# A decoder block in split fp32: weight preparation held back before three norms, transposes under the first loads, and pairs of matmuls in turned order

## Chip, core and metric

The kernel runs on one core of a Trainium2 chip. The metric is the device time of one execution in microseconds; three executions of the kernel before were timed, and one more was profiled. The engines are TensorE (PE in the profile, with its weight loads as PEld), VectorE (DVE), ScalarE (ACT), GpSimd (POOL) and SyncE (SP), which issues most of the DMAs. Each engine works through its own list of instructions in the order in which they were written.

## What is computed

One decoder block for 256 tokens of 2048 channels, all in fp32. Cut to its core, the reference is:

```
x = layer_norm(ALPHA * x + 0.5 * swiglu(x, ffn1_w_gate, ffn1_w_up, ffn1_w_down), ln1_g, ln1_b)
mix = hybrid_mixer(x, ...)            # x @ w_in, RG-LRU and dilated attention, @ w_out
x = layer_norm(ALPHA * x + mix, ln2_g, ln2_b)
x = layer_norm(ALPHA * x + 0.5 * swiglu(x, ffn2_w_gate, ffn2_w_up, ffn2_w_down), ln3_g, ln3_b)
x = x + sigmoid(x @ w_ple_gate) * (p @ w_ple_proj)
```

The hidden width of swiglu is 5632. There are three layer norms, and behind each of them a new large product starts that needs the normed x.

## The kernel before

**Split products.** Every large product is made of fp32r matmuls on split operands: a weight tile of 256 x 512 (an *entry* of the plan, `plan[q]`) is loaded as `raw`, ACT casts it to `hi` (L104), DVE subtracts to get `lo` (L109). The activations are split in the same way (`xT[:, :, 0]` and `xT[:, :, 1]`). An entry is 1.05 us of work on ACT and 1.2 us on DVE.

**Two forms of product.** With the weight stationary (`mm_stationary_w`), each 128 x 128 block gives a *pair*: `hi` against 512 columns (both halves of xT) and `lo` against 256. With the activations stationary (`mm_moving_w`), each block gives three matmuls of 512 columns.

**The plan.** `take` hands out the next entry; `advance` prepares entries ahead, at most 7 beyond those taken (`AHEAD`), at most `SLOTS` = 7 live at once, and never beyond `self.limit`. An entry that is marked `work` gets its `hi` and `lo` in the pool `work` (11 buffers, tag `w4`) and needs no slot. Two entries in `down_last` (`plan[-6:-4]`, those of its n = 1) and the first three entries behind each boundary are marked so. `advance` emits the cast of an entry, and its subtraction one entry later.

**A boundary.** `down_last` ends a stage. It makes its four column blocks n = 0..3 for the first 128 tokens (t = 0), where DVE adds each into `acc` (L385) and takes its statistics (`ln_stats`, L513), then `ln_norm(st[0], 0)` norms the first half (aggregate, a power on POOL, four scalings at L525). The four blocks for t = 1 follow on PE; in the middle of the one with n = 1, the first four normed blocks are transposed (`ln_transpose(0, 0)`, L535), and further transposes stand behind n = 1, 2 and 3. ACT scales and casts what was transposed (L538, L64), DVE subtracts (L65). Then the next stage starts on the first 128 tokens, with the transposes of the second half behind its entries j = 4 to 7 (`HOOKS`). The boundaries are here called LN1 (about 700 us), LN2 (about 1071 us) and LN3 (about 1780 us).

**The entries behind a boundary** are prepared while `down_last` takes its own. They are called W1, W2 and W3 below: they appear in the trace as `w<-raw` on ACT and `w<-raw,w` on DVE, in contrast to the `hi<-raw` and `lo<-raw,hi` of the entries in slots.

**The mixer.** In `group_a` the weight is stationary; between its entries `tick` steps the generators `lru` and `attention`, which put small groups of plain fp32 matmuls and transposes into PE's stream.

**The start.** SP loads the pieces of x and the first entries of `ffn1_w_gate`; POOL writes the identity for the transposes in `setup`.

Of the kernel before, what the change touches and what calls it, by code (L numbers as in the profile page):

```python
# [12 lines left out]
P = 128  # L13
D = 2048
S = 256
KB = D // P
# [24 lines left out]
class Block:  # L41
# [119 lines left out]
    def make_plan(self):  # L161
        i = self.i
        plan = self.plan = []

        def add(w, r0, c0, n=1, **kw):
            for j in range(n):
                plan.append({"src": self.rows2(w, r0 + 256 * j, c0), "work": False,
                             "parts": [slice(0, 2)], "stationary": False, **kw})

        def ffn(name):  # L170
            g, u, d = (i[f"{name}_w_{v}"] for v in ("gate", "up", "down"))
            todo = []
            for c in range(NCH):
                for w in (g, u):
                    for j in range(8):
                        add(w, 256 * j, c * 512, stationary=c > 0 or name == "ffn1")
                        if j % 2 and todo:
                            todo.pop(0)()
                if c % 2:
                    todo = blocks(d, (c - 1) * 512, 0)  # L180
                    if c < NCH - 2:
                        todo += blocks(d, (c - 1) * 512, 2)
            for n in (2, 3):
                add(d, (NCH - 3) * 512, n * 512, 4)
            last_down(d, (NCH - 1) * 512)

        def last_down(w, r0):
            down(w, r0)
            for e in plan[-6:-4]:
                e["work"] = True  # L190

        def blocks(w, r0, n):
            got = {}

            def entries(kind):
                for j in range(2):
                    entry(kind, j)

            def entry(kind, j):
                r, c = r0 + 256 * j, n * 512  # L200
                b22, b21 = self.rows2(w, r + 512, c + 512), self.rows2(w, r + 512, c)
                at = {"p2": (512, 0), "p3": (512, 512)}.get(kind, (0, 0))
                add(w, r + at[0], c + at[1], kind=kind)
                e = got[kind, j] = plan[-1]
                p1 = got["p1", j]
                if kind == "p1":
                    e["beside"] = self.rows2(w, r, c + 512)
                    e["after"] = [lambda: self.raw_sum(p1["raw"], p1["other"]), lambda: self.raw_grow(p1["other"], b22)]
                elif kind == "p3":
                    e["after"] = [lambda: self.raw_sum(p1["raw"], e["raw"])]  # L210
                elif kind == "p6":
                    e["after"] = [lambda: self.raw_grow(p1["raw"], b21)]
                if kind in ("p5", "p6", "p4", "p7"):
                    e["of"] = p1, "other" if kind == "p7" else "raw"

            return [lambda kind=kind: entries(kind) for kind in ORDER]

        def down(w, r0):
            for n in range(4):
                add(w, r0, n * 512, 2)  # L220

        w, wo = i["w_in"], i["w_out"]
        ffn("ffn1")
        for j in range(8):
            plan[j]["load"] = lambda j=j: self.load_x(j)
            plan[j]["split"] = lambda j=j: self.split_x(j)
            plan[16 + j]["load"] = lambda j=j: self.load_acc(j)
        plan[0]["parts"] = [slice(0, 1), slice(1, 2)]
        v0 = len(plan)
        add(w, 0, QW + KVW, 8)  # L230
        for g in range(3):
            add(w, 0, C_X + g * 512, 8, stationary=True)
        for h in range(4):
            add(w, 0, h * 512, 8)
        for g in range(3):
            add(w, 0, C_Y + g * 512, 8, stationary=True)
            down(wo, g * 512)
        last_down(wo, 3 * 512)
        f0 = len(plan)
        ffn("ffn2")  # L240
        p0 = len(plan)
        for n in range(4):
            add(i["w_ple_proj"], 0, n * 512)
        q = len(plan)
        for n in range(4):
            add(i["w_ple_gate"], 0, n * 512, 8)
        for e in plan[q + 6:q + 8] + plan[-2:]:
            e["work"] = True
        for q in (v0, f0, p0):
            for e in plan[q:q + 3]:  # L250
                e["work"] = True
        plan[p0]["load"], plan[p0]["split"] = self.load_p, self.split_p
        self.xraw = {}
        self.limit = len(plan)
        self.loaded = self.ready = self.ready_lo = self.taken = self.live = 0
        self.ticks = 0
        self.lru_q, self.att_q, self.gate_q, self.res_q, self.form_q = [], [], [], [], []

    def rows2(self, w, r0, c0):
# [3 lines left out]
    def mm(self, out, lhsT, rhs, start, stop):  # L263
        self.nc.tensor.matmul(out, lhsT=lhsT, rhs=rhs, start=start, stop=stop, skip_group_check=True)  # L264

    def mm_stationary_w(self, bank, b, hi, lo, k, kb, tok, start, stop):
        bv = bank.rearrange("p (s t) -> p s t", s=2)
        c = slice(b * P, (b + 1) * P)
        self.mm(bv[:, :, tok], hi[:, k, c], self.xT[:, kb, :, tok], start, False)
        self.mm(bv[:, 0, tok], lo[:, k, c], self.xT[:, kb, 0, tok], False, stop)  # L270

    def mm_moving_w(self, bank, act, hi, lo, start, stop):
        ah, al = act
# [8 lines left out]
    def tokens_a(self, e, j, banks, tok, first, on_block=None):  # L282
        for b in range(4):
            for k in range(2):
                kb = 2 * j + k
                self.mm_stationary_w(banks[b], b, e["hi"], e["lo"], k, kb, tok, kb == 0 and first, kb == KB - 1)
            if on_block and j == 7:
                on_block(b, banks[b])

# [201 lines left out]

    def down_last(self, acts):
        es, st = [], [self.tile(self.small, [P, 4, 6], F32, "bst") for _ in range(2)]
        for n in range(4):
            es.append([self.take(), self.take()])
            self.down_mm(acts, es[n], 0, n, False)
            self.ln_stats(st[0], 0, n)
        self.ln_norm(st[0], 0)
        for n in range(4):
            self.down_mm(acts, es[n], 1, n, False, mid=(lambda: self.ln_transpose(0, 0)) if n == 1 else None)  # L500
            self.ln_stats(st[1], 1, n)
            if n < 3:
                for e in es[n]:
                    self.done(e)
            if n > 0:
                self.ln_transpose(0, n)
        self.ln_norm(st[1], 1)
        for e in es[3]:
            self.done(e)
# [130 lines left out]
    def setup(self):  # L640
        nc, i = self.nc, self.i
        c = self.const
        self.ident = c.tile([P, P], F32, name="ident")
        make_identity(nc, self.ident)
        self.mhalf = c.tile([P, 1], F32, name="mhalf")
        nc.gpsimd.memset(self.mhalf, -0.5)
        self.par = c.tile([P, 192], F32, name="par")
        self.trig = c.tile([P, 2, 2, 16], F32, name="trig")
        self.dec = c.tile([P, 2, 12], F32, name="dec")
# [56 lines left out]
    def lru(self, g, xb):  # L706
        nc, i = self.nc, self.i
# [17 lines left out]
        for b in range(4):  # L725
            gb = 4 * g + b
            bank = self.bank()
            self.mm(bank[:, :256], wr[:, b, :], xc[:, b, :], True, True)
            self.mm(bank[:, 256:], wi[:, b, :], xc[:, b, :], True, True)
            nc.scalar.activation(r[:, b, :], bank[:, :256], AF.Sigmoid, bias=self.par[:, 60 + gb:61 + gb])  # L730
            nc.scalar.activation(ig[:, b, :], bank[:, 256:], AF.Sigmoid, bias=self.par[:, 72 + gb:73 + gb])
            if b % 2:
                yield
        nc.gpsimd.tensor_tensor(ig, ig, xc, op=ALU.mult)
        th = self.wide()
# [38 lines left out]
    def attention(self, h, qks):  # L774
        nc = self.nc
# [30 lines left out]
        for t in range(2):  # L806
            nc.vector.tensor_reduce(mxs[t], prs[t][:, :, :(t + 1) * P], AX.XY, ALU.max)
            nc.vector.tensor_scalar(mxs[t], mxs[t], -SCALE, None, op0=ALU.mult)
        yield
        for t in range(2):  # L810
            pv = prs[t][:, :, :(t + 1) * P]
# [13 lines left out]
        nc.tensor.transpose(bank[:, 2 * P:3 * P], ps[1][:, P:], self.ident)  # L825
        pT = self.tile(self.qk, [P, 3 * P], F32, "qk")
        nc.scalar.copy(pT, bank[:, :3 * P])
        yield
        ob = self.bank()
        hc = slice(h * P, (h + 1) * P)  # L830
# [1 line left out]
        self.mm(ob[:, P:2 * P], self.v[:, 0, hc], pT[:, P:2 * P], True, False)  # L832
        self.mm(ob[:, P:2 * P], self.v[:, 1, hc], pT[:, 2 * P:], False, True)
        nc.scalar.copy(self.att[0][:, h, :], ob[:, :256])
        yield
        nc.vector.tensor_tensor(self.att[1][:, h, :], ob[:, :256], self.att[0][:, h, :].bitcast(F32), op=ALU.subtract)

# [12 lines left out]
    def mixer(self):  # L850
        nc = self.nc
# [7 lines left out]
        for h in range(4):  # L859
# [5 lines left out]
                qks.append(qk)  # L865

            self.group_b(on_bank)
            if h == 0:
                self.att = (self.wide_r(), self.wide_r())
            self.att_q.append(self.attention(h, qks))  # L870
# [138 lines left out]
```

## Time and profile before

| what | value |
|---|---|
| timed runs | 1912.32 us median of 3 (1910.5 to 1912.78) |
| profiled execution | 1905.79 us, of which 1904.0 us from its first to its last instruction |
| PE busy | 1868.5 us, 98% of the span, 9844 matmuls |
| DVE busy | 1494.9 us, 79% |
| ACT busy | 1077.8 us, 57% |
| POOL busy | 124.2 us, 7% |
| TensorE's granted clock | 0.995 of full speed over the span |

The profile is of one execution, and the time of that execution stands beside its span; the 1.79 us between them lie around the instructions. Ends of matmuls are modelled, so the starts are the better guide. A wait is written as idle time in brackets with the engine and line that ended it.

### The profile page before, as it was taken

The numbers are of one execution on the slowest core, as the hardware profiler recorded it, in microseconds if no ns is written. First come the engines' busy times: TensorE is split into PE (matmuls) and PEld (weight loads), VectorE is DVE, ScalarE is ACT, GpSimd is POOL, SyncE is SP. The second block draws the span as 40 slices with busy tenths as digits, with TensorE's granted clock in tenths as the row PEclk, the third lists the DMA queues.
The fourth block names the chain that finished last, engine by engine and source line by source line (L and its number), as shares of the span: only waits on it lengthen the run. The fifth ranks groups of instructions, "written<-read, shape, count | busy, mean of one in ns | idle before, by whom it ended". The sixth has DMA issues, their size and how long they took to land.

```text
span 1904.0 us, 26424 instructions
## 1 busy us (share of the span) xinstructions
PE 1868.5 (98%) x9844; PEld 1603.2 (84%) x9844; DVE 1494.9 (79%) x1910; ACT 1077.8 (57%) x1422; POOL 124.2 (7%) x108
## 2 busy tenths in 40 slices
PE   8999999999999989999999899999999999999899
PEld 7888888888888878887888788888888888888687
DVE  6698887887888876688677867878879888788674
ACT  6565555555655646555755455655556556556552
POOL 0001010100010000011100000101000101010000
PEclk9999999999999999999999999999999999999999
DMA  9678687788786857565455575887887878778381
GB/s 354 232 198 264 203 257 235 207 260 247 211 255 209 266 178 231 175 185 158 138 184 187 167 243 155 250 231 211 258 247 207 255 211 253 243 198 276 131 263 44
DMA packets 214593, 413.02 MB, mean 217 GB/s; under 512 B 13104, under 2 KB 15808, under 8 KB 214464
## 3 DMA queue, kind: packets, MB, share of 16 engines
q1 hardware_dynamic: 193856, 370.42, 58.1%
q0 software_dynamic: 20608, 40.91, 12.6%
q8 instruction: 77, 1.26, 0.3%
q14 instruction: 52, 0.43, 0.1%
HBM read 409.18 MB, written 2.10 MB: 216 GB/s over the span
## 4 chain that ended last, share of the span: by engine, by line
PE 95%; DVE 2%; ACT 1%; issue 1%; DMA 0%; SPq 0%; POOL 0%; DVEq 0%; POOLq 0%; ACTq 0%
PE mm L264 94%; DVE lo L109 1%; PE mm L535 1%; DMA raw<-in_ffn_w_gate_dram 0%; ACT hi L104 0%; DVE w L109 0%; DVE bst L513 0%; DVE acc L385 0%; PE mm L792 0%; DVE raw L82 0%; DVE w L721 0%; DVE w L65 0%; ACT w L64 0%; POOL rs L522 0%; DVE w L627 0%
## 5 line engine op out<-in xcount | busy, mean ns | idle before, releaser
L104 ACT CAST hi<-raw 128x1024 fp32r<-128x1024 f32 (+1 forms) x774 | 797.2, 1049 | 556.4 <-PE mm L264 501.2
L264 PE MATMUL mm<-xT,hi 128*128 128x512 f32 x3072 | 1057.6, 391 | 5.6 <-ACT hi L104 5.6
L109 DVE TENSOR_TENSOR lo<-raw,hi 128x1024 fp32r<-128x1024 f32 (+1 forms) x774 | 915.2, 1221 | 93.4 <-ACT hi L104 84.5
L264 PE MATMUL mm<-xT,lo 128*128 128x256 f32 x3072 | 850.5, 277 | 0.1
L264 PEld LDWEIGHTS mm<-xT,hi 128*128 128x128 f32 x3072 | 577.5, 188 | 127.2 <-ACT hi L104 5.8
L264 PEld LDWEIGHTS mm<-xT,lo 128*128 128x128 f32 x3072 | 577.7, 188 | 6.3 <-DVE lo L109 1.3
L264 PE MATMUL mm<-hi,w 128*128 128x512 f32 x1480 | 481.6, 391 | 1.8 <-DVE acc L435 1.2
L264 PEld LDWEIGHTS mm<-hi,w 128*128 128x128 f32 x1480 | 277.9, 188 | 63.7 <-ACT hi L104 1.5
L264 PE MATMUL mm<-lo,w 128*128 128x512 f32 x740 | 289.5, 391 | 0.0
L264 PE MATMUL mm<-hi,xT 128*128 128x512 f32 (+1 forms) x648 | 200.9, 385 | 0.0
L264 PEld LDWEIGHTS mm<-lo,w 128*128 128x128 f32 x740 | 139.1, 188 | 23.9
L85 POOL DMA_DIRECT2D raw<-in_ffn_w_down_dram x72 | 86.6, 1214 | 1080.7 <-DVE raw L82 547.7
L437 DVE TENSOR_TENSOR acc<-acc,mm 128x512 f32<-128x512 f32 x110 | 75.2, 684 | 98.6 <-PE mm L264 98.6
L264 PEld LDWEIGHTS mm<-hi,xT 128*128 128x128 f32 x648 | 120.3, 188 | 23.1
L264 PE MATMUL mm<-lo,xT 128*128 128x512 f32 (+1 forms) x324 | 123.6, 382 | 0.0
L378 DVE TENSOR_TENSOR w<-mm,w 128x256 f32<-128x256 f32 x192 | 80.2, 419 | 20.5 <-ACT w L377 20.0
L82 DVE TENSOR_TENSOR raw<-raw,raw 128x1024 f32<-128x1024 f32 x72 | 87.9, 1221 | 1.2
L377 ACT COPY w<-mm 128x256 f32<-128x256 f32 x192 | 69.6, 364 | 21.2 <-PE mm L264 17.2
L64 ACT CAST w<-qk 128x512 fp32r<-128x512 f32 (+1 forms) x42 | 25.5, 609 | 86.4 <-DVE qk L482 46.0
L612 ACT ACTIVATE w<-w 128x256 f32<-128x256 f32 x84 | 35.1, 418 | 66.3 <-DVE w L378 66.3
L264 PEld LDWEIGHTS mm<-lo,xT 128*128 128x128 f32 x324 | 61.0, 188 | 11.2
L613 DVE TENSOR_TENSOR w<-w,w 128x256 f32<-128x256 f32 x84 | 35.8, 426 | 41.4 <-ACT w L612 41.4
(139 smaller groups left out, 788.0 us busy)
## 6 DMA issues: line engine op xcount, KB each, us to landing
raw<-in_ffn_w_up_dram SPq DMA_DIRECT2D x176, 512.0 KB, 4.9
raw<-in_ffn_w_down_dram SPq DMA_DIRECT2D x176, 512.0 KB, 5.3
raw<-in_ffn_w_gate_dram SPq DMA_DIRECT2D x175, 512.0 KB, 6.0
raw<-in_w_in_dram SPq DMA_DIRECT2D x88, 512.0 KB, 4.6
raw<-in_ffn_w_down_dram POOLq DMA_DIRECT2D x72, 512.0 KB, 7.6
raw<-in_w_out_dram SPq DMA_DIRECT2D x32, 512.0 KB, 4.4
raw<-in_w_ple_gate_dram SPq DMA_DIRECT2D x32, 512.0 KB, 5.6
w<-in_ln_g_dram SPq DMA_DIRECT2D x12, 256.0 KB, 7.4
```

What stands on the lines that cost most here:

```text
L64: self.nc.scalar.copy(hi, src)
L82: self.nc.vector.tensor_tensor(a, a, b, op=ALU.add)
L85: self.nc.gpsimd.dma_start(a, src, accum_op=ALU.add)
L104: self.nc.scalar.copy(e["hi"][:, k, :], e["raw"][:, k, :])
L109: self.nc.vector.tensor_tensor(e["lo"][:, k, :], e["raw"][:, k, :], e["hi"][:, k, :].bitcast(F32), op=ALU.subtract)
L264: self.nc.tensor.matmul(out, lhsT=lhsT, rhs=rhs, start=start, stop=stop, skip_group_check=True)
L377: self.nc.scalar.copy(c, bank[:, 256:])
L378: self.nc.vector.tensor_tensor(dst, bank[:, :256], c, op=ALU.add)
L437: self.nc.vector.tensor_tensor(a, a, bank, op=op)
L535: nc.tensor.transpose(bank[:, q * P:(q + 1) * P], self.acc[:, t, kb * P:(kb + 1) * P], self.ident)
L612: nc.scalar.activation(s, g, AF.Sigmoid)
L613: nc.vector.tensor_tensor(g, g, s, op=ALU.mult)
```

## The change

Three edits are independent of each other.

- In `down_last` the limit of the plan is set to ten entries from the one taken first (its own eight and two behind the boundary) until the norm of the first token half has been emitted; then it is set back.
- In `setup`, eight transposes of the identity into a PSUM bank that nothing reads are issued to PE ahead of everything else.
- In the mixer, a flag `turn` is set behind each group of fp32 matmuls in `lru` and behind three of the four groups of `attention`; the next pair with the weight stationary (and not the first of its bank) is then issued with `lo` first and `hi` second. The flag is dropped where a `group_b` ends.

```
+        self.limit = self.taken + 10
         for n in range(4):
             es.append([self.take(), self.take()])
             self.down_mm(acts, es[n], 0, n, False)
             self.ln_stats(st[0], 0, n)
         self.ln_norm(st[0], 0)
+        self.limit = len(self.plan)
...
         make_identity(nc, self.ident)
+        bank = self.bank()
+        for _ in range(8):
+            nc.tensor.transpose(bank[:, :P], self.ident, self.ident)
...
-        self.mm(bv[:, :, tok], hi[:, k, c], self.xT[:, kb, :, tok], start, False)
-        self.mm(bv[:, 0, tok], lo[:, k, c], self.xT[:, kb, 0, tok], False, stop)
+        high = bv[:, :, tok], hi[:, k, c], self.xT[:, kb, :, tok]
+        low = bv[:, 0, tok], lo[:, k, c], self.xT[:, kb, 0, tok]
+        one, two = (low, high) if turn else (high, low)
+        self.mm(*one, start, False)
+        self.mm(*two, False, stop)
...
-                self.mm_stationary_w(banks[b], b, e["hi"], e["lo"], k, kb, tok, kb == 0 and first, kb == KB - 1)
+                turn = self.turn and kb > 0
+                self.mm_stationary_w(banks[b], b, e["hi"], e["lo"], k, kb, tok, kb == 0 and first, kb == KB - 1, turn)
+                if turn:
+                    self.turn = False
```

On DVE, at LN1, the instructions around the first norm stand in this order before (`w_1283`, `w_1287` and `w_1290` are the `lo` of W1, W2 and W3, `acc<-acc,mm` are the additions of n = 1, 2 and 3, and `BN_AGGR` begins the norm):

```order
L109 TENSOR_TENSOR w_1283_6572<-raw_6505,w_1282_6571 128x1024
L109 TENSOR_TENSOR w_1287_6593<-raw_6523,w_1286_6592 128x1024
L385 TENSOR_TENSOR acc<-acc,mm_6602 128x512
L513 BN_STATS bst_6561<-acc 128x6
L109 TENSOR_TENSOR w_1290_6599<-raw_6541,w_1289_6598 128x1024
L385 TENSOR_TENSOR acc<-acc,mm_6623 128x512
L513 BN_STATS bst_6561<-acc 128x6
L385 TENSOR_TENSOR acc<-acc,mm_6638 128x512
L513 BN_STATS bst_6561<-acc 128x6
L518 BN_AGGR mv_6653<-bst_6561 128x2
L520 TENSOR_SCALAR ve_6655<-mv_6653 128x1
L525 TENSOR_SCALAR acc<-acc,mv_6653,rs_6657 128x512 x4
```

With the change the same stretch of DVE's list, from the statistics of n = 2 on, reads as follows (`w_1288` is the `lo` of W2, `w_1298` that of W3):

```order
L521 BN_STATS bst_6570<-acc 128x6
L391 TENSOR_TENSOR acc<-acc,mm_6635 128x512
L521 BN_STATS bst_6570<-acc 128x6
L526 BN_AGGR mv_6650<-bst_6570 128x2
L528 TENSOR_SCALAR ve_6652<-mv_6650 128x1
L533 TENSOR_SCALAR acc<-acc,mv_6650,rs_6654 128x512 x4
L391 TENSOR_TENSOR acc<-acc,mm_6660 128x512
L521 BN_STATS bst_6571<-acc 128x6
L109 TENSOR_TENSOR w_1288_6602<-raw_6532,w_1287_6601 128x1024
L109 TENSOR_TENSOR w_1298_6678<-raw_6550,w_1297_6677 128x1024
L109 TENSOR_TENSOR lo_6684<-raw_6572,hi_6683 128x1024
L109 TENSOR_TENSOR lo_6690<-raw_6578,hi_6689 128x1024
```

The subtractions of W2 and W3 have moved from between the additions of the first token half to behind the norm and the first addition of the second half. It is the same at LN2 and LN3. The lists of ACT, SP and POOL keep their order everywhere.

On PE, in the mixer's first group behind the fp32 matmuls of `lru` (`mm<-w,w`, 128x256), the stream before and now:

```order
L264 MATMUL mm_7394<-w_1403_7234,w_1402_7231 128x256 x2
L264 MATMUL mm_7399<-w_1403_7234,w_1402_7231 128x256 x2
L264 MATMUL mm_7205<-xT,hi_7227 128x512
L264 MATMUL mm_7205<-xT,lo_7228 128x256
L264 MATMUL mm_7205<-xT,hi_7227 128x512
L264 MATMUL mm_7205<-xT,lo_7228 128x256
```

```order
L264 MATMUL mm_7403<-w_1404_7243,w_1403_7240 128x256 x2
L264 MATMUL mm_7408<-w_1404_7243,w_1403_7240 128x256 x2
L264 MATMUL mm_7214<-xT,lo_7237 128x256
L264 MATMUL mm_7214<-xT,hi_7236 128x512 x2
L264 MATMUL mm_7214<-xT,lo_7237 128x256
```

One pair has its two matmuls exchanged, so that two of 512 columns follow each other once. This happens at six places of the stream: behind the three groups of `lru` matmuls that fall among pairs, and behind three groups of `attention`, all for the last head. The eight transposes of the identity are the first work of PE.

## Rows read from the trace of the kernel before

**Rows 1.** The page: the chain that ended last, shares of the span.

```profile
PE 95%; DVE 2%; ACT 1%; issue 1%; DMA 0%; SPq 0%; POOL 0%; DVEq 0%; POOLq 0%; ACTq 0%
```

**Rows 2.** Windows at LN1: busy us (instructions) by engine, PE clock, DMA share, GB/s.

```profile
700.00:707.00 7.00, 1.41 (x7) 0.91 (x6) 5.20 (x10) 0.76 (x1) 0.57 (x1) 0.72 0.27 75
707.00:717.00 10.00, 10.00 (x47) 8.29 (x46) 9.90 (x15) 7.32 (x16) 0.00 (x0) 0.86 0.32 107
```

**Rows 3.** Timeline of DVE at LN1: start, duration, engine, line, operation, idle before.

```profile
700.90 1.23 DVE L109 TENSOR_TENSOR w<-raw,w 128x1024 fp32r<-128x1024 f32 x1 [6.92 <-PE mm L264]
...
703.37 0.67 DVE L385 TENSOR_TENSOR acc<-acc,mm 128x512 f32<-128x512 f32 x1
...
706.01 1.92 DVE L525 TENSOR_SCALAR acc<-acc,mv,rs 128x512 f32<-128x512 f32 x4 [0.76 <-POOL rs L522]
707.84 0.68 DVE L385 TENSOR_TENSOR acc<-acc,mm 128x512 f32<-128x512 f32 x1
...
709.17 2.34 DVE L109 TENSOR_TENSOR lo<-raw,hi 128x1024 fp32r<-128x1024 f32 x2
711.43 0.68 DVE L65 TENSOR_TENSOR xT<-qk,xT 128x512 fp32r<-128x512 f32 x1
...
719.22 0.69 DVE L65 TENSOR_TENSOR xT<-qk,xT 128x512 fp32r<-128x512 f32 x1 [0.81 <-ACT xT L64]
...
720.94 1.92 DVE L525 TENSOR_SCALAR acc<-acc,mv,rs 128x512 f32<-128x512 f32 x4 [0.67 <-POOL rs L522]
```

**Rows 4.** Timeline of PE at LN1.

```profile
699.51 1.52 PE L264 MATMUL mm<-w,w 128*128 128x512 f32 x6
706.62 1.11 PE L535 MATMUL mm<-ident,acc 128*128 128x128 f32 x4 [5.59 <-DVE acc L525]
...
713.54 0.48 PE L264 MATMUL mm<-hi,w 128*128 128x512 f32 x1
...
716.75 4.36 PE L264 MATMUL mm<-w,xT 128*128 128x512 f32 x18
```

**Rows 5.** Timelines of PE at LN2 and LN3, and of DVE at LN3.

```profile
1070.25 1.52 PE L264 MATMUL mm<-w,w 128*128 128x512 f32 x6
1077.26 1.11 PE L535 MATMUL mm<-ident,acc 128*128 128x128 f32 x4 [5.49 <-DVE acc L525]
...
1088.06 4.38 PE L264 MATMUL mm<-w,xT 128*128 128x512 f32 x18
...
1779.25 1.52 PE L264 MATMUL mm<-w,w 128*128 128x512 f32 x6
1788.80 1.11 PE L535 MATMUL mm<-ident,acc 128*128 128x128 f32 x4 [8.03 <-DVE acc L525]
...
1798.86 3.45 PE L264 MATMUL mm<-w,w 128*128 128x512 f32 x14
...
1780.64 1.23 DVE L109 TENSOR_TENSOR w<-raw,w 128x1024 fp32r<-128x1024 f32 x1 [8.71 <-ACT hi L104]
```

**Rows 6.** The chain that ended last, 0 to 30 us: start, duration, what.

```profile
2.69 6.48 DMA raw<-in_ffn_w_gate_dram
...
11.54 18.64 PE mm L264 x108
```

**Rows 7.** PE's timeline around an fp32 group; groups by form, 782.86:809.8 and 930.66:969.8.

```profile
780.64 0.39 PE L264 MATMUL mm<-xT,hi 128*128 128x512 f32 x1
...
780.98 0.39 PE L264 MATMUL mm<-xT,hi 128*128 128x512 f32 x1
...
791.07 0.39 PE L264 MATMUL mm<-xT,hi 128*128 128x512 f32 x1
...
791.42 0.39 PE L264 MATMUL mm<-xT,hi 128*128 128x512 f32 x1
...
L264 PE MATMUL mm<-xT,hi 128*128 128x512 f32 x72 | 25.7, 400 | 0.0
...
L264 PE MATMUL mm<-xT,hi 128*128 128x512 f32 x41 | 14.9, 403 | 0.0
```

More of the change, by code (lines that the diff above doesn't have):

```diff
@@ L255, in make_plan @@
         self.loaded = self.ready = self.ready_lo = self.taken = self.live = 0
-        self.ticks = 0
+        self.ticks, self.turn = 0, False
         self.lru_q, self.att_q, self.gate_q, self.res_q, self.form_q = [], [], [], [], []
@@ L264, in mm, with mm_stationary_w @@
         self.nc.tensor.matmul(out, lhsT=lhsT, rhs=rhs, start=start, stop=stop, skip_group_check=True)
-    def mm_stationary_w(self, bank, b, hi, lo, k, kb, tok, start, stop):
+    def mm_stationary_w(self, bank, b, hi, lo, k, kb, tok, start, stop, turn=False):
         bv = bank.rearrange("p (s t) -> p s t", s=2)
         c = slice(b * P, (b + 1) * P)
-        self.mm(bv[:, :, tok], hi[:, k, c], self.xT[:, kb, :, tok], start, False)
-        self.mm(bv[:, 0, tok], lo[:, k, c], self.xT[:, kb, 0, tok], False, stop)
+        high = bv[:, :, tok], hi[:, k, c], self.xT[:, kb, :, tok]
[3 more added lines that the diff above has]
+        self.mm(*two, False, stop)
     def mm_moving_w(self, bank, act, hi, lo, start, stop):
@@ L732, in lru @@
             if b % 2:
+                self.turn = True
                 yield
@@ L808, in attention @@
             nc.vector.tensor_scalar(mxs[t], mxs[t], -SCALE, None, op0=ALU.mult)
+        self.turn = True
         yield
@@ L827, in attention @@
         nc.scalar.copy(pT, bank[:, :3 * P])
+        self.turn = True
         yield
@@ L834, in attention @@
         nc.scalar.copy(self.att[0][:, h, :], ob[:, :256])
+        self.turn = True
         yield
@@ L867, in mixer @@
             self.group_b(on_bank)
+            self.turn = False
             if h == 0:
```

## Prediction

> **What bounds the kernel now.** I read the page's chain first: PE holds 95% of it [rows 1], so time is to be had only where PE stands still or runs slowly. The list of PE's longest idle times came next. Three stand out, one at each norm: 5.59, 5.49 and 8.03 us, each ended by DVE's scaling of `acc` [rows 4, 5]. The windows show what follows such a wait: the granted clock averages 0.72 in 700 to 707 us and 0.86 in 707 to 717 [rows 2], so PE also works at the lower of its two levels (1.2 instead of 2.4 GHz) for a time after it has stood still.
>
> DVE's timeline at LN1 says why the norm is late. From its idle time of 6.92 us on, DVE stands in front of one instruction, the `lo` of W3, until 700.90 [rows 3]; the additions of n = 2 and 3 and the norm are behind it in DVE's list, though PE had long finished those blocks. What W3 waits for is PE, in the six matmuls that begin at 699.51 [rows 4]: the second pass over the entries with n = 1. The pool `work` explains it: 11 buffers, of which the two tiles of activations, the four of the entries with n = 1 and the six of W1 to W3 would need twelve. So PE waits for the norm, the norm for W3, and W3 for a buffer that PE releases only just before it has to stop. At LN3 one tile more is in use (that of `p`), and there already W2 is held, for 8.71 us; its row names ACT, but the time is that of the same six matmuls plus their latency [rows 5], and I take PE to be the releaser there too.
>
> **The boundaries.** The change leaves W1 in its place and moves the `lo` of W2 and W3 behind the norm; ACT, SP and POOL keep their order. Durations are those of the profiled execution.
>
> - When is the norm ready? PE steps 0.227 us per matmul of 512 columns: six take 1.52, less the 0.39 of the last, over five steps [rows 4]. The block of 12 ahead of the six began 2.72 us before 699.51, at 696.8, and there the first token half was complete. With 0.4 for the result to be released (one recorded matmul) the last addition starts at 697.2. From there to the scaling are 2.64 us (703.37 to 706.01), and 0.61 more until a transpose can start (706.01 to 706.62) [rows 3, 4]: 700.4. PE arrives at the transposes at 699.51 + 6 x 0.227 = 700.9. The wait is gone, with half a microsecond in hand.
> - What does PE save? A block of 12 and the transposes behind it take 716.75 - 713.54 = 3.21 us at the full clock [rows 4]; a half block with transposes is 1.36 less, 1.85. From 699.51 the next stage thus starts 1.85 + 1.85 + 3.21 + 3.21 = 10.12 us later, at 709.63 instead of 716.75: 7.12 us. The same reckoning gives 1088.06 - 1080.37 = 7.69 at LN2 and 1798.86 - 1789.37 = 9.49 at LN3 [rows 4, 5]. The sum is **24.3 us**. It contains the clock: with no long stop it should not fall, which is what remains after the idle time itself (1.4 us at LN1).
> - What is late next? DVE. Between 707 and 717 it is busy 9.90 of 10 us [rows 2], and it now has two subtractions more there, 2.26 us (709.17 to 711.43) [rows 3]. Before, the first scaling and that of the second token half lie 14.93 us apart (706.01 to 720.94), 0.81 of it a wait for ACT [rows 3]; with the 2.26 they are 16.4 apart. From 697.2 + 2.64 = 699.8 the second norm then begins at 716.2 and gives its first quarter at 716.8. PE wants it behind the entries j = 0 to 4, 30 matmuls after 709.63, at 716.4: a wait of 0.4 us at LN1, and as much at LN2; at LN3 the products with `p` lie between, and there is none. The first piece of xT is ready at 699.8 + 5.42 + 2.26 + 0.68 = 708.2 (706.01 to 711.43, the moved work, its own length), ahead of 709.63. The `lo` of the entry j = 6 follows the second norm at 716.2 + 1.83 + 1.21 = 719.2, about when PE gets to it. I subtract **0.8 us**. If the 2.26 us lay bare at all three, it would be 6.8; if none, 0.
> - Loads: W2's raw buffer is freed some 11 us later, so a load into it, which SP holds in its list, starts later. In 700 to 717 the DMA share is 0.27 to 0.32 [rows 2], and what it feeds lies beyond the eight entries of the group, more than 20 us on. I cost it at nothing.
>
> **The turned pairs.** A pair takes 780.98 - 780.64 = 0.34 us before an fp32 group and 791.42 - 791.07 = 0.35 behind one [rows 7], and it stays at 0.35 until a run of 512-column matmuls comes. 72 and 41 pairs stand in the two stretches concerned [rows 7], so about 113 x 0.01 = 1.1 us are to be had if the exchange, which puts one 512 behind another, brings the faster step back, and 0 if not. No row shows a single such neighbour; I take half, **0.6 us**. [...]
>
> **The transposes at the start.** The chain runs through a load that lands at 9.17 (2.69 + 6.48), the second entry's, and through its cast and subtraction to PE at 11.54 [rows 6]. Transposes under the loads, four of which take 1.11 us even at the lower clock [rows 4], are over long before; should they raise the clock earlier, PE finishes the first entry sooner and waits longer for the second. I cost them at nothing; neither a gain nor a loss has a way past that load.
>
> **Sum.** -24.3 + 0.8 - 0.6 = -24.1 us. The profiled execution goes from 1905.79 to 1881.7 (span 1904.0 to 1879.9). The median of the timed runs lies 6.5 above the profiled one, and I let that stand: **1888.2 us**, 1.3% faster. A measurement of this kernel tells about 0.2% (3.8 us) from no change.
>
> **Rivals.**
>
> - *The pairs stay slow.* For it: in the mixer the step of 0.35 at 791.07 stands behind the second fp32 group of its stretch, which found it slow and left it so [rows 7]. Everything else as above: 1888.8. I give 0.38; it lies inside the range.
> - *DVE becomes the bound.* The 2.26 us of moved work come out as PE's wait at each boundary, before the second half's transposes or before an entry. For it: DVE is full there, and my margins are 0.4 us and less. Against it: all of that work but the 2.26 shifts forward with the norm by more than 6 us. The sum loses 6.8 instead of 0.8: 1894.2. Chance 0.11.
> - *The change does not free the norm.* The additions of n = 2 and 3 may themselves get word from PE only with the six matmuls, as W3 did; then only the moved work goes from in front of the norm, 1.13 us (half of 2.26) at LN1 and LN2 and twice that at LN3: 4.5 us, 1907.8, near the edge of what can be measured. Against it: the addition of n = 1 and those before the boundary run as soon as their block ends. Chance 0.05.
> - *Slower.* The stop moves to the transposes of the second half and grows: PE waits there, the clock falls in the middle of the new stage, and every matmul after it pays. To end 3.8 us above before, the three boundaries must lose 28.1 us, 9.4 each, so the second norm would have to begin at about 726 instead of 716.2. That needs 10 us of DVE work or waits that no row shows. About 1917. Chance 0.03.
>
> **Range and chances.** The forecast has 0.43 and the first rival 0.38; both lie in 1885 to 1891, with 24.3 + 1.1 - 0 as the lower bound (1886.9) and two microseconds for the runs, whose own spread is 2.3. With the second rival the range is 1884 to 1895, which holds some 0.88 by the mechanism and 0.8 with what I may have overlooked. Faster 0.94 (all but the slow case and half of the third rival), same 0.04, slower 0.02.
>
> **What would show it.** Right: no idle time over 1 us in front of PE's transposes at the three norms; a granted clock of 1.00 in the windows there; W2 and W3 on DVE behind the scaling and without idle time; the next stage's first matmul about 10.1 us after the six; pairs at 0.34 behind the turned ones; PE's second entry still starting at about 11.5. Wrong: an idle time of DVE in front of the additions of n = 2 or 3, PE waiting at the transposes of j = 4 for several microseconds, or a clock that falls although PE does not stop.

## The result, and the profile after

| what | before | after |
|---|---|---|
| timed runs beside each other | 1911.41 us median of 4 (1909.25 to 1912.78) | 1885.33 us median of 4 (1884.09 to 1885.8) |
| profiled execution | 1905.79 us, span 1904.0 | 1885.8 us, span 1884.0 |
| granted clock over the span | 0.995 | 0.999 |

The ratio is 0.9864, with a 95% interval of 0.9846 to 0.9881: 1.4% faster, 26.08 us by the medians. Over the 27 runs of before that were made beside the first four experiments its median is 1910.08 (1906.53 to 1912.93), and against these the change gives 24.75 us. In the two profiled executions the spans differ by 20.0 us only, 4.1 less than the 24.1 that were forecast; where these went is a question below.

The page's chain after the change, which answers to [rows 1]:

```profile
PE 97%; DVE 1%; ACT 1%; issue 0%; DMA 0%; SPq 0%; ACTq 0%; DVEq 0%
```

The windows at LN1 after, with the columns of [rows 2]:

```profile
700.00:707.00 7.00, 7.00 (x36) 5.83 (x35) 6.10 (x12) 4.83 (x9) 0.57 (x1) 1.00 0.00 0
707.00:717.00 10.00, 10.00 (x49) 8.24 (x49) 9.90 (x14) 7.48 (x16) 0.00 (x0) 1.00 0.69 218
```

PE is busy for all of the 17 us and the clock is 1.00, where it had been 0.72 and 0.86. DVE's timeline at LN1 after, which answers to [rows 3]:

```profile
693.05 1.21 DVE L109 TENSOR_TENSOR w<-raw,w 128x1024 fp32r<-128x1024 f32 x1
...
699.73 0.69 DVE L391 TENSOR_TENSOR acc<-acc,mm 128x512 f32<-128x512 f32 x1 [1.30 <-PE mm L264]
...
702.39 1.92 DVE L533 TENSOR_SCALAR acc<-acc,mv,rs 128x512 f32<-128x512 f32 x4 [0.76 <-POOL rs L530]
...
705.55 2.34 DVE L109 TENSOR_TENSOR w<-raw,w 128x1024 fp32r<-128x1024 f32 x2
...
718.68 1.92 DVE L533 TENSOR_SCALAR acc<-acc,mv,rs 128x512 f32<-128x512 f32 x4 [0.67 <-POOL rs L530]
```

The additions now wait only 1.30 us for PE's blocks, as they should. W2 and W3 stand behind the scaling (705.55, two of them, no idle time). PE's timeline at LN1, LN2 and LN3 after, which answers to [rows 4, 5]:

```profile
702.25 1.53 PE L264 MATMUL mm<-w,w 128*128 128x512 f32 x6
703.61 0.60 PE L543 MATMUL mm<-ident,acc 128*128 128x128 f32 x4
...
712.20 4.38 PE L264 MATMUL mm<-w,xT 128*128 128x512 f32 x18
...
718.91 0.39 PE L264 MATMUL mm<-hi,xT 128*128 128x512 f32 x1
719.29 0.66 PE L543 MATMUL mm<-ident,acc 128*128 128x128 f32 x4
...
1066.22 1.53 PE L264 MATMUL mm<-w,w 128*128 128x512 f32 x6
...
1076.19 2.09 PE L264 MATMUL mm<-w,xT 128*128 128x512 f32 x8
...
1768.92 1.53 PE L264 MATMUL mm<-w,w 128*128 128x512 f32 x6
...
1778.87 1.41 PE L264 MATMUL mm<-w,w 128*128 128x512 f32 x5
```

Neither row of transposes has idle time in brackets. From the six matmuls to the next stage are 9.95, 9.97 and 9.95 us; in [rows 4, 5] they were 17.24, 17.81 and 19.61. But the six at LN1 start at 702.25, and before they started at 699.51: the change lost 2.74 us on the way there.

### The profile page after: what moved, and what is told of

Same layout as the page of the kernel before. It is cut to its first block, busy times and chain, and to the rows that moved or that the text cites. A ratio compares the mean times of both kernels' runs of the same rounds, so it can differ in the third digit from the quotient of the medians.

```text
span 1884.0 us, 26440 instructions
## 1 busy us (share of the span) xinstructions
PE 1870.2 (99%) x9852; PEld 1603.7 (85%) x9852; DVE 1494.4 (79%) x1910; ACT 1077.3 (57%) x1422; POOL 124.2 (7%) x108
## 4 chain that ended last, share of the span: by engine, by line
PE 97%; DVE 1%; ACT 1%; issue 0%; DMA 0%; SPq 0%; ACTq 0%; DVEq 0%
PE mm L264 96%; PE mm L543 1%; DVE lo L109 1%; DMA raw<-in_ffn_w_gate_dram 0%; ACT hi L104 0%; PE mm L804 0%; DVE w L732 0%; DVE raw L82 0%; DVE w L65 0%; ACT w L64 0%; DVE w L635 0%; DVE w L384 0%; ACT L755 0%; ACT L825 0%; ACT w L754 0%
## 5 line engine op out<-in xcount | busy, mean ns | idle before, releaser
L264 PEld LDWEIGHTS mm<-lo,xT 128*128 128x128 f32 x324 | 61.0, 188 | 11.5
```

## The parts one by one

Each experiment is made from the kernel before, and compared with runs of before on the same chip.

**The limit alone**

```
+        self.limit = self.taken + 10
...
         self.ln_norm(st[0], 0)
+        self.limit = len(self.plan)
```

> The kernel before with the edit of the limit alone. Theory (the prediction's): all of the gain is made at the three boundaries, 24.3 us less 0.8 for DVE, so 23.5 us below the kernel before (ratio 0.9877), no idle time over 1 us in front of the transposes at the three norms and the granted clock at 1.00 there. Rival: the change gained 26.1 us in the medians because the transposes at the start or the turned pairs give something too; then this kernel stays 2.6 us or more above the changed kernel, near 1888.

1885.73 us (1883.87 to 1886.61, 4 runs), ratio 0.987 [0.9856, 0.9883]. That is 24.35 below before and not to be told from the whole change. PE's timeline has the same three boundaries:

```profile
703.26 1.53 PE L264 MATMUL mm<-w,w 128*128 128x512 f32 x6
704.63 0.60 PE L537 MATMUL mm<-ident,acc 128*128 128x128 f32 x4
...
713.21 1.17 PE L264 MATMUL mm<-w,xT 128*128 128x512 f32 x4
```

9.95 us from the six to the next stage, as in the whole change. The theory holds: the gain is the limit's.

**The eight transposes alone**

```
+        bank = self.bank()
+        for _ in range(8):
+            nc.tensor.transpose(bank[:, :P], self.ident, self.ident)
```

> The kernel before with the eight transposes alone. Theory: nothing (within 1 us), since the start is bound by the load of the second entry. Rival 1: the transposes steady the start and give the 2.6 us by which the medians fell more than the boundaries explain. Rival 2: they cost. In the trace of the changed kernel the first 264 pairs step at 0.35 us and more, 3.5 us in all over 0.34, and in the trace of before at 0.34; if the transposes are the cause, this kernel is 3.5 us slower (ratio 1.002) and its pairs before 100 us are at 0.35 in the profile.

1909.51 us (11 runs), ratio 1.0001 [0.9992, 1.001]: nothing, in either direction. Its profile has the first pairs at 0.35 (3.5 us over 0.34 in all), as rival 2 has it, but the price does not appear in the time, and the next two kernels show that the slow step is there without the transposes too.

**The turned pairs alone** (the flag and the exchange of the diff, without the rest)

> The kernel before with the turned pairs alone. Theory (the prediction's sum): 0.6 us faster, up to 1.1, with pairs at 0.34 behind the turned ones. Rival (the prediction's first): nothing, and the 113 pairs stay at 0.35 behind each group, as the trace of the changed kernel already has them.

1909.52 us (11 runs), ratio 0.9998 [0.9989, 1.0006]: no gain. The trace is finer than the time. From the first pair behind LN1 to the six matmuls at LN2 this profile needs 330.01 us and that of the whole change 330.01; the profile of before needs 329.74, and ten others without turned pairs 329.60 to 329.81. Turning **costs** some 0.27 us. PE's timeline of the whole change at the first turned pair shows that the step stays slow:

```profile
775.67 0.39 PE L264 MATMUL mm<-xT,hi 128*128 128x512 f32 x1
...
776.69 0.39 PE L264 MATMUL mm<-xT,hi 128*128 128x512 f32 x1
...
777.03 1.89 PE L264 MATMUL mm<-w,w 128*128 128x256 f32 x8
778.57 0.47 PE L264 MATMUL mm<-xT,lo 128*128 128x256 f32 x1
778.88 0.63 PE L264 MATMUL mm<-xT,hi 128*128 128x512 f32 x2
779.35 0.28 PE L264 MATMUL mm<-xT,lo 128*128 128x256 f32 x1
779.46 0.40 PE L264 MATMUL mm<-xT,hi 128*128 128x512 f32 x1
...
781.92 0.39 PE L264 MATMUL mm<-xT,hi 128*128 128x512 f32 x1
```

Ahead of the group three pairs take 1.02 us (775.67 to 776.69), 0.340 each; behind the two 512s that now follow each other (the row of two at 778.88) seven take 2.46 (779.46 to 781.92), 0.351 each. The cost arises in the two longest stretches behind a turned pair: from start to end 56 pairs take 19.97 us and 24 take 8.66, in this profile and in that of the turned pairs alone, where before needs 19.78 and 8.59. The first rival of the prediction was right, and the turned pairs are slightly worse than it had them.

**Before again**, unchanged

> The kernel before, unchanged, for a second profile. Its timed runs lie 3.5 to 7 us above its first profiled execution (1905.79). Theory: that execution was a favourable one in its pairs: a stretch of pairs falls to the step of 0.35 or to 0.34 by chance in each execution, at the start (264 pairs, 3.5 us) and behind the eight transposes at 1137 us (135 pairs, 1.35 us). Then a profile at 1909 to 1912 has the first stretch or both at 0.35, and one at 1906 has neither. Rival: the pairs step as before and the difference lies at the boundaries (longer waits, a longer time at the lower clock) or in the loads.

1909.16 us (11 runs), ratio 0.9995 [0.9987, 1.0004], span of the profiled execution 1906.2. Its pairs step at 0.34 in both stretches, as in the first profile. Its 2.2 us over the first come from elsewhere: 0.9 from the start, where the first pairs ran at half clock to 12.5 us instead of 10.1, and 1.2 at the boundaries, where from the six matmuls on it needs 0.7, 0.3 and 0.1 us more than [rows 4, 5] for the same work behind the same waits. So here the rival is right. The other profiles show the step of the pairs as a second source: the kernel with the turned pairs alone, whose instructions before 100 us are those of before, has the first pairs at 0.35, and its profile is 5.1 us longer than the first. No kernel was profiled at both steps, so a rival is that the step goes with the kernel and not with the execution. The times speak against it: outside the boundaries that kernel's profile has 3.5 us more than this second profile of before (1.97 up to LN1, 0.20 up to LN2, 1.37 up to LN3), which would be a ratio of 1.0019, and the interval of its 11 runs ends at 1.0006.

## Why the wait was there, and what it cost

**The limit at eleven** (`self.taken + 11`)

> The kernel before with the limit at eleven entries instead of ten: W1 and W2 are split ahead of the norm, and of W3 the cast too; only the subtraction of W3 comes behind it. Theory (eleven buffers, of which PE's six matmuls release two): at LN1 and LN2 the two tiles of activations, the four of the entries with n = 1, the four of W1 and W2 and the hi of W3 are eleven, so DVE finds its buffers and the wait there is gone as with ten; at LN3 one tile more is in use, so the lo of W2 waits again, the norm with it, and PE stands about 8 us. Gain about 7.0 + 7.7 = 14.7 us, 1895.4 (ratio 0.992). Rival 1: it is enough that W3 is behind the norm, and the gain is that of ten, 24.4 us. Rival 2: buffers are not the cause, and the first entry moved behind the norm gives a third of it at each boundary.

1894.06 us (1893.1 to 1894.36), ratio 0.9914 [0.9899, 0.993]: 17.0 below before. At LN1 and LN2 the boundary is that of ten entries. At LN3, PE's timeline and then DVE's:

```profile
1768.53 1.52 PE L264 MATMUL mm<-w,w 128*128 128x512 f32 x6
1776.94 1.11 PE L537 MATMUL mm<-ident,acc 128*128 128x128 f32 x4 [6.89 <-DVE acc L527]
```

```profile
1769.92 1.22 DVE L109 TENSOR_TENSOR w<-raw,w 128x1024 fp32r<-128x1024 f32 x1 [8.71 <-ACT hi L104]
...
1776.34 1.92 DVE L527 TENSOR_SCALAR acc<-acc,mv,rs 128x512 f32<-128x512 f32 x4 [0.75 <-POOL rs L524]
```

The `lo` of W2 waits for 8.71 us, as it did in [rows 5], again until shortly after the six matmuls begin, and only at the boundary where one tile more is in use. W3, whose subtraction alone was moved, no longer counts. This is what eleven buffers ask for. The row names ACT, but in the trace DVE's wait for PE's semaphore ends at 1769.88, just ahead of the 1769.92 at which the `lo` begins; in the profile of before it ends at 1780.59 there (and at 700.85 at LN1), each time 0.05 us behind the modelled end of the fifth of the six matmuls. So PE is the releaser at LN3 too, as the prediction took it to be. From the six to the end of the traced stretch LN3 gains 0.9 us here, against 9.7 with ten.

**The limit at nine** (`self.taken + 9`)

> The kernel before with the limit at nine entries: W1, W2 and W3 are all subtracted behind the norm. Theory (DVE is full behind the norm, the prediction's second rival): 1.2 us more of DVE's work there at each boundary comes out as waits of PE, up to 3.5 us in all: 1889 against 1885.7 with ten. Rival: DVE has room, and it is 1885.7.

1887.42 us (1886.91 to 1888.17), ratio 0.9881 [0.9863, 0.9899], 1.7 above the limit at ten. PE's timeline has two new waits, at the transposes of the second token half:

```profile
719.96 0.66 PE L537 MATMUL mm<-ident,acc 128*128 128x128 f32 x4 [1.15 <-DVE acc L527]
...
1084.60 0.65 PE L537 MATMUL mm<-ident,acc 128*128 128x128 f32 x4 [1.06 <-DVE acc L527]
```

There is none at LN3, so of the 3.5 us expected some 2.3 came in the trace. One subtraction more of 1.2 us behind the norm comes out nearly whole at LN1 and LN2. So the mechanism of the prediction's second rival exists, and ten entries lie at its edge: with them PE waits about 0.15 us at the same place (718.91 + 0.227 = 719.14 against 719.29 in the rows of after).

**PE kept at work in the stop**

```
+        bank = self.bank()
+        for _ in range(32 if self.which == 2 else 22):
+            self.mm(bank, acts[0][:, 0, :P], acts[0][:, 0:2, :], True, True)
         self.ln_transpose(0, 0)
```

> The kernel before, in which PE fills its stop at the three norms with 22, 22 and 32 matmuls of 512 columns whose result nothing reads (5.0, 5.0 and 7.3 us at 0.227 each, within the stops of 5.59, 5.49 and 8.03); the wait itself stays. Theory: of the gain of 24.8 us up to the next stage's first matmul 19.6 are the stop and 5.2 the lower clock behind it (1.5 at LN1, 2.2 at LN2, 1.5 at LN3), so this kernel keeps the clock at 1.00 and is 5.2 us faster than before: 1904.9 (ratio 0.9973). Rival 1: the clock falls for another reason, and nothing is won. Rival 2: the stops set the time behind them otherwise (DVE's backlog), and the clock's return is worth less than 2 us.

1902.32 us (1901.61 to 1905.19, 5 runs), ratio 0.9961 [0.9946, 0.9976]. PE's timeline at LN1, and the window there:

```profile
702.77 1.52 PE L264 MATMUL mm<-w,w 128*128 128x512 f32 x6
704.13 5.15 PE L264 MATMUL mm<-w 128*128 128x512 f32 x22
709.89 0.66 PE L541 MATMUL mm<-ident,acc 128*128 128x128 f32 x4 [0.60 <-DVE acc L531]
```

```profile
700.00:717.00 17.00, 16.40 (x78) 13.31 (x78) 11.87 (x19) 8.47 (x17) 0.57 (x1) 1.00 0.23 68
```

The transposes come 7.12 us after the six, as before (706.62 - 699.51 = 7.11), so the wait is untouched; the clock stays at 1.00. From the six to the first pair behind the boundary (at LN3, to PE's last matmul) the profile needs 1.48, 2.19 and 1.42 us less than that of before: 5.09, where 5.2 were expected. That is the share of the clock; of the 24.4 us that the change saves over the same stretches, the other 19.3 are the stop itself. Against the three other profiles with the old limit the clock's share is 5.7 to 6.6 us. The timed gain is 8.8 us by the medians, 4.6 to 10.3 by the interval; the trace's lies within.

**Every second pair turned** (with the limit at ten)

```
-  ... kb == 0 and first, kb == KB - 1)
+  ... kb == 0 and first, kb == KB - 1, k == 1)
```

> The kernel with the limit at ten alone, and in the products with the weight stationary every second pair turned (hi lo, lo hi, hi lo, ...), so that matmuls of 512 columns stand two by two, and those of 256 too; some 2900 pairs. Theory 1 (order is worth nothing): 0.340 a pair as before, or 0.35 where it was 0.35; 1885.7. Theory 2 (the idea of turning is right, but one turned pair is too few): all pairs leave the step of 0.35, about 5 us of the slow stretches come back, 1881. Theory 3 (two matmuls of 256 columns in a row are too short for their weight loads of 0.188 us): a pair of 256s takes 0.376 instead of 0.227, 0.15 for every two pairs, 220 us slower.

1925.92 us (1925.87 to 1927.26), ratio 1.0084 [1.0068, 1.0099]: 40.2 above the limit alone, 13.1 ns for each of the 3072 pairs. None of the three theories. PE's timeline in the first product:

```profile
29.73 0.41 PE L264 MATMUL mm<-xT,lo 128*128 128x256 f32 x2
29.98 0.63 PE L264 MATMUL mm<-xT,hi 128*128 128x512 f32 x2
30.45 0.41 PE L264 MATMUL mm<-xT,lo 128*128 128x256 f32 x2
```

Two pairs take 0.72 us (29.73 to 30.45): 0.36 a pair, everywhere. In this order PE never gets to 0.34, so turning pairs is no way out of the slow step.

## The start, and a version with steadier times

**Matmuls of 512 columns in place of the transposes** (with the limit at ten; `z` is a tile of zeros)

```
+        for _ in range(8):
+            self.mm(bank, z[:, :P], z[:, 512:], True, True)
```

> The kernel with the limit at ten alone, and ahead of everything eight matmuls of 512 columns on a tile of zeros (nothing reads the result) where the change has eight transposes. Theory (at the start only the clock's rise and the step of the pairs are open, and transposes of 128 columns moved neither): PE works without a pause from about 1.7 us to the first pair, the granted clock rises ahead of the 10.1 to 13.3 us of the profiles so far, PE gets to the second entry before its split is there, and the rest of the stage starts when that is ready, at about 11.5; this is worth 0.5 to 1.2 us against the limit alone, 1884.5 to 1885.2, and up to 2.3 more where the pairs happen to step at 0.34. Rival: the rise comes with the pairs, as it did behind the transposes, and it is 1885.7.

1884.34 us (1884.27 to 1884.56), ratio 0.9865 [0.9851, 0.988]: 1.4 below the limit alone, inside the range of the latter's runs but with a tenth of their spread. PE's timeline at the start:

```profile
1.99 3.55 PE L264 MATMUL mm<-w 128*128 128x512 f32 x8 [1.99 <-DVE w L647]
5.38 0.46 PE L264 MATMUL mm<-xT,hi 128*128 128x512 f32 x1
...
7.59 0.40 PE L264 MATMUL mm<-xT,hi 128*128 128x512 f32 x1
...
11.24 0.39 PE L264 MATMUL mm<-xT,lo 128*128 128x256 f32 x1 [0.76 <-DVE lo L109]
```

The first matmul of a pair takes 0.46 at 5.38, and 0.40 from 7.59 on, so the full clock is there with the first pairs, and PE now stands in front of the second entry. With the change's transposes it is not:

```profile
1.37 1.97 PE L655 MATMUL mm<-ident 128*128 128x128 f32 x8 [1.37 <-POOL mhalf L657]
5.15 0.77 PE L264 MATMUL mm<-xT,hi 128*128 128x512 f32 x1 [1.81 <-DVE xT L65]
...
10.69 0.63 PE L264 MATMUL mm<-xT,hi 128*128 128x512 f32 x1
...
11.78 0.40 PE L264 MATMUL mm<-xT,hi 128*128 128x512 f32 x1
```

They are over at 3.34, and the matmuls of 0.63 go on to 11.3 (10.8 with the transposes alone); in the nine profiles with nothing ahead of the pairs they end between 10.1 and 13.6. The rows do not show whether it is the kind of work that makes the difference: the transposes also ended 1.8 us ahead of the pairs and the matmuls did not, and in the next kernel the same eight matmuls raise the clock no earlier than the transposes.

**Ten more of them between the first and the second entry**

> As the one before, and ten more such matmuls of 512 columns between the first and the second entry of the first product. Theory: a run of 512s puts PE into the step of 0.34 (every stretch of pairs that follows one is at 0.34 in all profiles), and there PE waits for the second entry anyway if the clock rose early; the 264 pairs before 100 us take 3.5 us less, of which some 1.2 come back as waits at 102 and 120 us, so about 1882.5. Rival: the run costs its own 2.3 us in front of the pairs and only exchanges it, 1885 to 1886; or the pairs fall to 0.35 all the same.

1885.62 us (1883.44 to 1886.23), ratio 0.9869 [0.9852, 0.9885]. PE's timeline:

```profile
1.99 3.78 PE L264 MATMUL mm<-w 128*128 128x512 f32 x8 [1.99 <-DVE w L655]
...
10.92 0.63 PE L264 MATMUL mm<-xT,hi 128*128 128x512 f32 x1
...
11.89 2.46 PE L264 MATMUL mm<-w 128*128 128x512 f32 x10
...
14.54 0.39 PE L264 MATMUL mm<-xT,hi 128*128 128x512 f32 x1
...
16.92 0.39 PE L264 MATMUL mm<-xT,hi 128*128 128x512 f32 x1
```

Behind the run the pairs are at 0.34 (seven from 14.54 to 16.92) up to 100 us, so such a run can reset the step. But it costs 2.3 us in front of them, and PE waits 0.6 us more behind: the six at LN1 start at 702.31, as in the changed kernel (702.25). The rival holds. In this execution the same eight matmuls did not raise the clock before 11.5.

That every stretch behind such a run is at 0.34 in all profiles, as was expected, is not so. PE's timeline of before:

```profile
102.42 0.73 PE L264 MATMUL mm<-hi,w 128*128 128x512 f32 x2 [0.59 <-DVE w L65]
...
104.84 0.39 PE L264 MATMUL mm<-xT,hi 128*128 128x512 f32 x1
...
106.24 0.40 PE L264 MATMUL mm<-xT,hi 128*128 128x512 f32 x1
```

Twelve matmuls of 512 columns stand ahead of these pairs, ten of them behind the wait, and four pairs still take 1.40 us (104.84 to 106.24), 0.35 each, though the pairs ahead of the twelve were at 0.34.

**The limit at 11, 11 and 10**

> The limit at eleven entries for LN1 and LN2, at ten for LN3. Theory (buffers): no wait at any of the three, as with ten, and one subtraction less behind the norm where DVE is full: from the six matmuls to the first pairs 33.75 and 55.49 us, as with eleven, against 34.0 and 55.7, and 110.4 at LN3: 0.4 us in the sum, 1885.3, not to be told from ten in the time, only in the trace. Rival: a stop comes back at one of them, 5 us and more.

1884.61 us (1883.64 to 1885.61), ratio 0.9867 [0.9852, 0.9881]. From the six matmuls to the first pairs 33.71 and 55.49 us, and 110.38 at LN3: as expected, and too little to see in the time.

**Both**, with twelve matmuls at the start

> The limit at 11, 11 and 10 entries, and twelve matmuls of 512 columns ahead of everything instead of eight. Theory: eight of them raised the clock at 5.15 us in one profile and not before 11.51 in another, where PE had two waits between the first pairs; twelve last to about 6.5 to 7.3 us and cover these waits, so the clock rises before 9 us in each execution, the second entry's split still sets the time (11.2 us), and it is 0.3 us (from the limits) to 1 us faster than the 1884.34 of eight matmuls with ten: 1883.3 to 1884.0. Rival: the first pairs are only put off by 1.5 us and the second entry is reached later than it is ready: 1885.

1884.32 us (1884.04 to 1884.63), ratio 0.9862 [0.9845, 0.9878]. PE's timeline:

```profile
1.99 5.33 PE L264 MATMUL mm<-w 128*128 128x512 f32 x12 [1.99 <-DVE w L647]
7.16 0.40 PE L264 MATMUL mm<-xT,hi 128*128 128x512 f32 x1
...
11.03 0.39 PE L264 MATMUL mm<-xT,lo 128*128 128x256 f32 x1 [0.67 <-DVE lo L109]
```

The clock is full at the first pair, and the split of the second entry sets the time, as expected; the 1883.3 to 1884.0 us expected from it did not come, and the sum is that of eight matmuls. This is the best version of the study, 1.0 us below the changed kernel by the medians, within the latter's range (1884.09 to 1885.8): not shown to be faster, only steadier.

## Why the prediction was right, point by point

The forecast was 1888.2 us (1884 to 1895) and a change of -24.1; measured were 1885.33, and -26.08 against the four runs of before beside them or -24.75 against 27.

- **The wait and its cause**: right. W3's `lo`, and at LN3 W2's, waited for buffers that PE's six matmuls release. The limits at ten, eleven and nine tell this from the rivals; a kernel with more buffers was not run.
- **The boundaries, 24.3**: right. From the six to the next stage the profiles save 7.29, 7.84 and 9.66, together 24.8; the 10.12 us that were reckoned are 9.96.
- **DVE's backlog, 0.8**: right in place, too large. To the first pairs (at LN3, to the last matmul) 7.03, 7.69 and 9.66 are saved, 24.4, so 0.4 is lost. The second norm's scaling begins 16.29 us behind the first (702.39 to 718.68), where 16.4 were reckoned.
- **The clock**: right. The falls are gone and are worth 5.1 us of it, measured by the filled stop; at LN1 1.48, where 1.4 were reckoned.
- **The turned pairs, -0.6**: wrong. The step that failed is "the exchange, which puts one 512 behind another, brings the faster step back". One such neighbour does not; a run of ten did at the start of one kernel, and runs of twelve do throughout the first product but for the stretch at 105 us shown above. The term is +0.27.
- **The start, 0**: right in the time (ratio 1.0001), for too strong a reason. That "neither a gain nor a loss has a way past that load" holds only if PE reaches the second entry early. It came there at about the time its split was ready, and the moment at which the clock rises and the step of the pairs then move the start of the six at LN1 between 699.5 and 703.3 us, with transposes and without.
- **The base**: "The median of the timed runs lies 6.5 above the profiled one, and I let that stand" was the larger error. Of the 2.9 us between forecast and time 2.2 are the base (1912.32, the median of three runs, against 1910.08 of 27) and 0.65 the change. The profiled execution was forecast at 1881.7 and came to 1885.8, 4.1 higher, and the changed kernel's median lies 0.5 below its profiled time instead of 6.5 above. That these two errors largely cancel is luck; the boundaries are not. The first profile of before lies low: full clock at about 10.1, pairs at 0.34 at the start and behind the eight transposes that follow LN2, and short boundaries: the three other profiles that have the old limit and no filled stop need 0.6, 1.2 and 1.5 us more there. In the five profiles with ten at all three boundaries the same stretches agree within 0.05 us, which fits with the timed runs lying closer together.

With this the 20.0 us between the two profiles come out: -24.38 at the boundaries, +2.74 ahead of LN1 (264 pairs with 3.5 us more and the clock 1.4 us later, against waits of PE at 11 and 102 us that fell away), +0.27 for the turned pairs, and +1.39 between LN2 and LN3 (135 pairs behind eight transposes, at 0.35 instead of 0.34): -19.98. The second and the last belong to no one edit: the limit alone has both (3.75 and 1.43), the turned pairs alone have both (2.86 and 1.41), and the times of the latter show no such price. Against the other three profiles of before's boundaries the gain there is 25.0 to 25.9, near the 24.75 of the medians; the timed runs themselves have no trace, so this last step is argued.

## What to carry to other kernels

A DVE instruction that waits for a buffer holds back whatever is behind it in DVE's list; count the buffers at a boundary before looking for a slow engine, and move such work behind what PE is waiting for, but no more of it than the engine has room for (here one 1.2 us subtraction too many already came out at PE). One profiled execution is one draw: before a sum is put on a median, see how far the timed runs lie from the profile, and whether the same stretch steps alike in a second profile.

## What the runs showed of the hardware

- A stretch of `hi`, `lo` pairs runs at 0.340 or at 0.35 us a pair, and keeps its step until something else comes between. Behind twelve or more matmuls of 512 columns at the full clock with no wait among them it was at 0.34 in every profile; with a wait of 0.6 us ahead of the last ten, at about 105 us, it was at 0.35 in both profiles of before and at 0.34 in the one other that has it; behind fp32 matmuls nearly always at 0.35; behind eight transposes of `w` at 0.34 in 3 of 13 profiles and at 0.35 in 10; at the start at 0.34 in 2 of the 12 profiles with nothing between the first two entries (the kernel with every second pair turned is left out of all these counts). What decides it there stays open: the instructions were the same in most of them.
- In the order hi lo, lo hi the pair takes 0.36.
- After a stop of 5.5 to 8 us at the norms PE ran at half clock for a time, and that cost 1.4 to 2.7 us in the four profiles with the old limit; filled with matmuls, the same stop left the clock at 1.00.
